# Building the second mixer's bias tables from GpSimd's queue in the second feed-forward block instead of from SyncE's in the first

## The chip, the cores and the metric

The kernel runs on one core of a Trainium2 chip. The metric is the device time of one execution in microseconds; before the change it is 2590.12 us, the median of three runs (2588.21 to 2591.35).

A core has five engines that run side by side, each taking its own instructions in a fixed order: TensorE (PE, with its weight loads as PEld), VectorE (DVE), ScalarE (ACT), GpSimd (POOL) and SyncE (SP), which here only starts transfers. Sixteen DMA engines move the data. A transfer is started by an instruction in the queue of SyncE, ScalarE or GpSimd, and an engine that comes to an instruction whose input has not arrived waits, with everything behind it.

## What is computed

A trunk of two layers over 768 tokens (512 of a prompt, 256 of a sample) of width 1024, all in float32:

```python
def swiglu(h, wg, wu, wd):
    return (jax.nn.silu(h @ wg) * (h @ wu)) @ wd

def even_layer(x, ...):
    x = x + 0.5 * swiglu(rmsnorm(x, f1_n), f1_g, f1_u, f1_d)
    x = x + mixer_ab(rmsnorm(x, mix_n), ...)     # gMLP gate and windowed attention
    return x + 0.5 * swiglu(rmsnorm(x, f2_n), f2_g, f2_u, f2_d)

def odd_layer(x, ...):                           # the same two feed-forward blocks
    ...
    x = x + mixer_c(rmsnorm(x, mix_n), w_qkv, rpb, w_out)
    ...

def neighbourhood_attn(q, k, v, rpb):
    ...
    dr = rs + jnp.arange(kh) - r + (NA_KH - 1)
    bias = rpb[:, dr][:, :, dc]
    s = jnp.einsum('bchd,bacjhd->bhcaj', q_row, k_win) * (HEAD_DIM ** -0.5)
    s = s + jnp.transpose(bias, (0, 2, 1, 3))[None]
    ...
```

The hidden width of the feed-forward blocks is 2816. The second mixer attends to a neighbourhood in a grid of 64 columns and adds a relative position bias `rpb` (16 heads, 15 x 31 values). The bias depends only on an input of the program, not on anything computed.

## The kernel before

**Stages.** `build` runs six phases one after the other: the feed-forward blocks l0f1, l0f2, l1f1 and l1f2, and between them the first mixer (after l0f1) and the second (after l1f1). In the profiled execution l0f1 runs until about 520 us, the first mixer to about 805, l0f2 to about 1260, l1f1 to about 1740 and the second mixer to about 2130.

**A feed-forward block** (`ffn`) takes the hidden width in 11 pairs of 256 columns (numbered 0 to 10). Each product of two matrices is made as seven products of half-size blocks, of sums and differences of the blocks, in place of eight. The sums of weight blocks are made on VectorE (`sums`, line 739, tile `s`). Every weight block then becomes a rounded part `whi` and a remainder `wlo` (`wsplit`, lines 122 and 123, on ScalarE and VectorE), and three matrix products (line 152) take the place of one in full precision. The order of a block is: the first two products of pairs 0 to 3, then the rest of pair 0, 1, 2 and so on. After pair 2 comes `down` for pairs 0 and 1, the product with the down weights, whose results are accumulated into `x` by VectorE (line 795); then pairs 3 and 4, `down` for 2 and 3, and so on.

**Weights** are loaded by `raw` (line 107) in tiles of 512 KB, from SyncE's queue, into four buffers. A load can start once an earlier tile in the same buffer has been read for the last time. For pairs 0 to 3 of each block, one of the weight sums is built by the transfers themselves: `added` starts two loads into the same tile `s` on GpSimd's queue, the second of which adds to what the first has written (`accum_op`). There are 16 such loads in each block, 8 plain and 8 accumulating.

**The bias tables.** The second mixer wants the bias laid out by query position. `bias_tables` (line 1621) builds that with transfers from DRAM to DRAM, in two steps for the prompt and two for the sample: 16 shifted copies of `rpb` into `skew`, 8 strided copies from `skew` into `tab`, then 32 and 4 of the same for the sample, 60 in all. A copy into `skew` moves 16 x 15 pieces of 32 or 48 numbers (30 or 45 KB); a copy into `tab` moves 16 x 16 pieces of 1 KB or 16 x 32 pieces of 768 bytes. `bias_tables` does not start them; it puts them on a list, `spare`, when `build` comes to the first phase. `raw` starts one of them, on SyncE's queue, behind each weight load from the twentieth on (lines 108 and 109), so all of them stand among the loads of l0f1. What were left of the list would be started ahead of the second mixer (lines 1710 and 1711). `mixer1` reads the tables head by head (line 1423).

**What sets the order.** TensorE's instructions are in the order of the program, written out by hand. Those of the other engines are ordered by Tile's planner when the kernel is built, from priorities and from when it expects their operands to be there. `issue_after(ins)` puts what is traced within it behind `ins` on that engine's queue. `mixed` is true in the feed-forward blocks that follow a mixer, l0f2 and l1f2.

Of the kernel before, what the change touches and what calls it, by code (L numbers as in the profile page):

```python
# [55 lines left out]
class Trunk:  # L56
# [42 lines left out]
    def raw(self, name, k0, nk, c0, n, raw=None, eng=None, **kw):  # L99
        i = len(self.units)  # L100
        self.units.append((name, k0, nk, c0, n))
        size = P * nk * n
        src = self.aps["w"][self.woff : self.woff + size].rearrange("(p f) -> p f", p=P)
        self.woff += size
        if raw is None:
            raw = self.rawp.tile([P, nk * n], F32, tag="raw", name=f"raw{i}")
        (eng or self.nc.sync).dma_start(raw, src, **kw)  # L107
        if self.spare and i >= 20:
            self.spare.pop(0)()
        return raw.rearrange("p (k n) -> p k n", k=nk)  # L110

    def wsplit(self, src, eng=None, keep=False):
# [365 lines left out]
    def ffn(self, pre):  # L478
# [4 lines left out]
        mixed = bool(self.unfed)  # L483
# [229 lines left out]
        for p in range(NPAIR):  # L713
            for _ in stages[p]:
                pass
            if p == 2:
                acc += [self.fw.tile([P, H], F32, tag=f"p1{j}", name=f"p1{j}") for j in range(4)]
            if p and p % 2 == 0 and p < NPAIR - 1:
                self.down(pre, range(p - 2, p), d, acc, addeds.get(p + 1))
            if p == NPAIR - 2:  # L720
                self.down(pre, range(p - 1, p), d, acc)
        kind = self.following[0]
# [898 lines left out]
    def bias_tables(self):  # L1621

        dma = self.nc.sync.dma_start
        rpb = self.aps["rpb"]
        self.tabs = []
        for nc_, nr, ns in ((16, 8, 32), (32, 4, 48)):
            skew = self.dram.tile([nc_, 16, 15, ns], F32, tag=f"skew{ns}", name=f"skew{ns}")
            tab = self.dram.tile([16, P, nr * ns], F32, tag=f"tab{ns}", name=f"tab{ns}")  # L1630
            self.tabs.append(tab)
            for c in range(nc_):
                self.spare.append(
                    lambda skew=skew, c=c, ns=ns: dma(skew[c], rpb[:, :, RPB_PAD + 7 - c : RPB_PAD + 7 - c + ns])
                )
            for r in range(nr):
                src = skew.rearrange("c h d s -> h c (d s)")[:, :, (7 - r) * ns : (7 - r + nr) * ns]
                dst = tab.rearrange("h (c r) f -> h r c f", r=nr)[:, r]
                self.spare.append(lambda dst=dst, src=src: dma(dst, src))

    def build(self):
        nc = self.nc
        space = self.cp.tile([P, 96], F32, tag="space", name="space")
        todo = [KIND[p] for p in self.phases] + [("last", 6)]
        kind = todo[0][0]
        self.ident = self.cp.tile([P, P], F32, tag="ident", name="ident")
        self.ones = self.cp.tile([P, P], F32, tag="ones", name="ones")
        self.onesr = self.cp.tile([P, P], F32R, tag="onesr", name="onesr")
        if kind == "f":
            pre = f"{self.phases[0][:2]}_ffn{self.phases[0][3]}_w_"  # L1650
            raws = [self.rawp.tile([P, KD * P], F32, tag="raw", name=f"first{i}") for i in range(4)]
            self.first += [t.rearrange("p (k n) -> p k n", k=KD) for t in raws]

            def first(i, k, eng=None):
                name = pre + ("gate", "up")[i % 2]
                self.raw(name, 4 * k, 4, i // 2 * 2 * P, P, raws[i][:, k * 512 : k * 512 + 512], eng)

            first(0, 0, nc.scalar)
        nc.gpsimd.memset(self.ones, 1.0)
        nc.vector.tensor_copy(self.onesr, self.ones)  # L1660
        self.space = space
        self.silu()
        make_identity(nc, self.ident)
        self.gains = self.cp.tile([P, 64], F32, tag="gains", name="gains")[:, : KD * len(NORMS)]
        nc.scalar.dma_start(self.gains, self.aps["gains"])
        self.ngains = self.cp.tile([P, 64], F32, tag="ngains", name="ngains")[:, : KD * len(NORMS)]
        nc.gpsimd.tensor_scalar(out=self.ngains, in0=self.gains, scalar1=-1.0, scalar2=None, op0=ALU.mult)
        self.x = [self.xp.tile([P, T], F32, tag=f"x{m}", name=f"x{m}") for m in range(KD)]
        if kind == "f":
            self.ffn_open("right")  # L1670
            self.ffn_tiles()
            self.fw = self.open("work", "left")
            self.early = {}
            for h in (0, 1):
                self.spawn(self.tok_norm(h))
        elif kind != "last":
            self.mixer_tiles("right")
        self.norm_begin(todo[0])
        self.mixed = False
        if kind == "f":  # L1680
            ps = self.psum(self.aux, "aux")
            for _ in range(WARM):
                nc.tensor.matmul(ps[:, :P], lhsT=self.onesr, rhs=self.onesr, start=True, stop=True)
        for h, (c0, c1) in enumerate(HALVES):
            for m in range(KD):
                nc.sync.dma_start(self.x[m][:, c0:c1], self.aps["x"][m, :, c0:c1])
                if kind == "f":
                    if h == 0:
                        self.feed(m, 0)
                else:  # L1690
                    self.final(m, c0, c1)
                if h == 0 and m % 4 == 3 and kind == "f":
                    for i in range(4):
                        if m > 4 or i:
                            first(i, m // 4)
            if kind == "f":
                for _ in range(TOKQ[h]):
                    self.tok_load()
                if h:
                    self.spawn(self.second())  # L1700
            elif kind == "last":
                self.half_done(h)
            if kind == "last":
                self.drain()
        for i, ph in enumerate(self.phases):
            self.following = todo[i + 1]
            if i == 0 and "l1m" in self.phases:
                self.bias_tables()
            if ph == "l1m":
                while self.spare:  # L1710
                    self.spare.pop(0)()
            if ph == "l0m":
                self.mixer0()
            elif ph == "l1m":
                self.mixer1()
            else:
                self.ffn(f"{ph[:2]}_ffn{ph[3]}")
        self.drain()
        for n in list(self.guards)[::-1]:
            self.close(n)  # L1720
# [105 lines left out]
```

## Time and profile before

| | us |
|---|---|
| median of three runs | 2590.12 |
| lowest and highest | 2588.21, 2591.35 |
| the profiled execution, its time | 2590.38 |
| the profiled execution, its span (first to last instruction) | 2588.6 |

The mean granted TensorE clock of the profiled execution is 0.996 of full speed. Its page gives the busy time of each engine over the whole span, and the mean hides what single stages do: the first block, which holds the transfers in question, has to be read by itself, in a table of windows, in the chain of work that ended last, and in the timelines of single engines. In a timeline row stand the start, the length, the engine, the line, the operation, what it writes and reads, and in brackets the idle time ahead of it with the work that ended it.

### The profile page before, as it was taken

How to read it: one execution, taken by the hardware profiler on the slowest of the kernel's cores; microseconds unless marked ns; L12 is line 12 of the kernel's file. 1: busy time of each engine (PE TensorE's matmuls, PEld its weight loads, DVE VectorE, ACT ScalarE, POOL GpSimd, SP SyncE). 2: the span in 40 equal slices, each digit the busy share in tenths (PEclk: the TensorE clock that was granted, in tenths of full speed). 3: DMA queues.
4: the chain of work that ended last, by engine and by line, in shares of the span. 5: the costliest groups of instructions: out<-in, count | busy, mean ns of one | idle time of the engine just before them, and what ended most of it. 6: DMA issues, size and time to landing. Idle time of an engine off the chain costs nothing.

```text
span 2588.6 us, 41317 instructions
## 1 busy us (share of the span) xinstructions
PE 2552.2 (99%) x15114; PEld 2487.2 (96%) x15114; DVE 2232.6 (86%) x4662; ACT 1366.6 (53%) x2869; POOL 155.5 (6%) x252
## 2 busy tenths in 40 slices
PE   8999999999999999999999999999999999999998
PEld 8999999988899999999999999998998999999997
DVE  7988898978879989889998889886776699888897
ACT  7544454646656545445654445454455575444543
POOL 1000000000021000000100000001222220000000
PEclk9999999999999999999999999999999999999999
DMA  7523222331144322222542222242221343222222
GB/s 246 170 81 106 72 74 74 124 100 46 58 125 132 114 66 74 74 66 98 136 109 82 66 77 71 66 145 64 64 64 41 106 134 119 82 74 74 71 66 76
DMA packets 93372, 238.68 MB, mean 92 GB/s; under 512 B 21488, under 2 KB 34288, under 8 KB 93168
## 3 DMA queue, kind: packets, MB, share of 16 engines
q1 hardware_dynamic: 85712, 218.96, 26.3%
q0 software_dynamic: 7168, 16.78, 3.1%
q8 instruction: 119, 1.95, 0.3%
q14 instruction: 85, 0.70, 0.1%
q10 hardware_dynamic: 288, 0.29, 0.0%
HBM read 226.56 MB, written 15.07 MB: 93 GB/s over the span
## 4 chain that ended last, share of the span: by engine, by line
PE 89%; DVE 6%; ACT 2%; DMA 1%; issue 1%; SPq 0%; DVEq 0%; ACTq 0%
PE ps_mm L152 54%; PE ps_aux L152 34%; PE ps_aux L156 1%; DVE wlo L123 1%; ACT p L1109 1%; DVE p L1103 1%; DMA raw<-in_w 1%; DVE tl L209 0%; DMA x<-in_x 0%; DVE tmp L415 0%; DVE p L1119 0%; ACT whi L122 0%; DVE s L739 0%; DMA first<-in_w 0%; DVE o L1254 0%
## 5 line engine op out<-in xcount | busy, mean ns | idle before, releaser
L122 ACT CAST whi<-s 128x512 fp32r<-128x512 f32 x496 | 304.6, 620 | 407.3 <-DVE s L739 177.6
L122 ACT CAST whi<-raw 128x512 fp32r<-128x512 f32 x504 | 306.1, 619 | 222.9 <-PE ps_mm L152 91.3
L123 DVE TENSOR_TENSOR wlo<-s,whi 128x512 fp32r<-128x512 f32 x496 | 336.8, 684 | 61.0 <-ACT whi L122 53.4
L123 DVE TENSOR_TENSOR wlo<-raw,whi 128x512 fp32r<-128x512 f32 x471 | 321.7, 691 | 18.2 <-ACT whi L122 14.5
L152 PE MATMUL ps_mm<-db,whi 128*128 128x384 f32 x864 | 219.2, 334 | 0.0
L152 PE MATMUL ps_aux<-dt,whi 128*128 128x384 f32 x864 | 219.2, 334 | 0.0
L152 PEld LDWEIGHTS ps_aux<-dt,whi 128*128 128x128 f32 x864 | 156.0, 188 | 0.0
L152 PEld LDWEIGHTS ps_mm<-db,whi 128*128 128x128 f32 x864 | 156.0, 188 | 0.0
L152 PE MATMUL ps_mm<-xh,whi 128*128 128x512 f32 (+1 forms) x416 | 146.2, 352 | 0.0
L152 PE MATMUL ps_aux<-dt,wlo 128*128 128x384 f32 x432 | 144.4, 334 | 1.4 <-DVE wlo L123 1.4
L152 PE MATMUL ps_mm<-db,wlo 128*128 128x384 f32 x432 | 144.3, 334 | 0.0
L152 PE MATMUL ps_mm<-xh,wlo 128*128 128x512 f32 (+1 forms) x416 | 141.3, 340 | 0.0
L152 PE MATMUL ps_mm<-xl,whi 128*128 128x512 f32 (+1 forms) x416 | 141.2, 339 | 0.0
L739 DVE TENSOR_TENSOR s<-raw,raw 128x512 f32<-128x512 f32 x124 | 84.0, 685 | 25.7 <-DMA raw<-in_w 25.5
L578 DVE TENSOR_TENSOR u<-ps_aux,u 128x384 f32<-128x384 f32 x176 | 96.9, 550 | 4.9 <-PE ps_aux L152 4.8
L152 PE MATMUL ps_aux<-dh,whi 128*128 128x384 f32 x384 | 97.5, 334 | 0.0
L795 DVE TENSOR_TENSOR x<-ps_aux,x 128x384 f32<-128x384 f32 x160 | 85.3, 551 | 14.1 <-PE ps_aux L152 13.8
L1109 ACT ACTIVATE p<-p,st 128x256 f32<-128x256 f32 (+3 forms) x144 | 68.9, 480 | 49.3 <-DVE st L1107 49.2
L573 ACT COPY u<-ps_mm 128x384 f32<-128x384 f32 x176 | 83.5, 475 | 16.5 <-PE ps_mm L152 15.9
L795 DVE TENSOR_TENSOR x<-ps_mm,x 128x384 f32<-128x384 f32 x160 | 86.1, 550 | 7.1 <-PE ps_mm L152 6.8
L107 POOL DMA_DIRECT2D s<-in_w x64 | 47.1, 781 | 702.2 <-PE ps_aux L152 387.6
L152 PEld LDWEIGHTS ps_mm<-xh,whi 128*128 128x128 f32 x416 | 79.8, 192 | 9.3 <-issue 0.9
(516 smaller groups left out, 8134.1 us busy)
## 6 DMA issues: line engine op xcount, KB each, us to landing
raw<-in_w SPq DMA_DIRECT2D x346, 512.0 KB, 3.7
s<-in_w POOLq DMA_DIRECT2D x64, 256.0 KB, 5.0
xdm<-x SPq DMA_DIRECT2D x16, 384.0 KB, 2.4
x<-in_x SPq DMA_DIRECT2D x16, 192.0 KB, 6.3
tok<-in_xt SPq DMA_DIRECT2D x12, 256.0 KB, 6.5
xold<-xdm SPq DMA_DIRECT2D x8, 384.0 KB, 3.1
x<-xdm SPq DMA_DIRECT2D x8, 384.0 KB, 4.7
out_y<-y SPq DMA_DIRECT2D x8, 384.0 KB, 2.4
```

Source lines behind the costliest of these rows:

```text
L107: (eng or self.nc.sync).dma_start(raw, src, **kw)
L122: nc.scalar.copy(hi, src)
L123: (eng or nc.gpsimd).tensor_tensor(out=lo, in0=src, in1=hi.bitcast(F32), op=ALU.subtract)
L152: self.nc.tensor.matmul(out, lhsT=lhsT, rhs=rhs, start=start, stop=stop, **kw)
L156: self.nc.tensor.transpose(out, src, self.ident)
L573: nc.scalar.copy(e[n, out], bank[key, n])
L578: nc.vector.tensor_tensor(out=t, in0=bank[key, n], in1=t, op=ALU.add)
L739: f = lambda o, x, y, op: self.nc.vector.tensor_tensor(out=o, in0=x, in1=y, op=op)
L795: nc.vector.tensor_tensor(out=o, in0=ps, in1=o, op=ALU.add)
L1103: nc.vector.tensor_tensor_reduce(out=outs[i], in0=ps_list[i], in1=adds[i], scale=1.0, scalar=init[i], op0=ALU.add, op1=ALU.max, accum_out= ...
L1109: ins = nc.scalar.activation(outs[i], outs[i], AF.Exp, bias=nm[:, i : i + 1], accum_out=sm[:, i : i + 1])
```

## The change

```diff
@@ raw
-        (eng or self.nc.sync).dma_start(raw, src, **kw)
-        if self.spare and i >= 20:
-            self.spare.pop(0)()
+        ins = (eng or self.nc.sync).dma_start(raw, src, **kw).ins
+        if kw:
+            self.added = ins
         return raw.rearrange("p (k n) -> p k n", k=nk)
@@ ffn, in the loop over the pairs
             if p and p % 2 == 0 and p < NPAIR - 1:
                 self.down(pre, range(p - 2, p), d, acc, addeds.get(p + 1))
+                if mixed and p == 2 and self.spare:
+                    with self.tc.issue_after(self.added):
+                        while self.spare:
+                            self.spare.pop(0)()
@@ bias_tables
-        dma = self.nc.sync.dma_start
+        dma = self.nc.gpsimd.dma_start
@@ build
-            if ph == "l1m":
-                while self.spare:
-                    self.spare.pop(0)()
```

`raw` no longer starts transfers of the list; it keeps the last accumulating load in `self.added` (only such a load has a `kw`). In the first block with `mixed` true, which is l0f2, the whole list is started in one go behind the `down` of pairs 0 and 1, on GpSimd's queue and there behind the last accumulating load of pair 3, the last that the block has. The loop ahead of the second mixer goes. The 60 transfers themselves, what they read and write and their order among each other stay as they are; a copy into `tab` still waits for the copies into `skew` that it reads.

## The prediction

> **What bounds the kernel now.** I read the first part of the page, then the groups, for the engines and the price of a transfer on GpSimd's queue.
>
> ```profile
> span 2588.6 us, 41317 instructions
> PE 2552.2 (99%) x15114; PEld 2487.2 (96%) x15114; DVE 2232.6 (86%) x4662; ACT 1366.6 (53%) x2869; POOL 155.5 (6%) x252
> ...
> L107 POOL DMA_DIRECT2D s<-in_w x64 | 47.1, 781 | 702.2 <-PE ps_aux L152 387.6
> ```
>
> TensorE is busy for 2552.2 of 2588.6 us, so a change without TensorE work can only gain where TensorE stands still or runs slowly. The next view, of the two tiles `skew` and `tab`, says where the moved transfers are now and when their product is first read.
>
> ```profile
> L1634 SPq DMA_DIRECT2D skew<-in_rpb x48: 490/604/782, 42.7 to 227.3; - x48
> L1639 SPq DMA_DIRECT2D tab<-skew x12: 531/562/751, 76.5 to 272.9; - x12
> ...
> L1423 SPq DMA_DIRECT2D ba<-tab x16: 320/326/468, 1739.5 to 1961.6; - x16
> ```
>
> There are 60 transfers, issued between 42.7 and 272.9 us, all inside the first feed-forward block (l0f1), and the tables are first read at 1739.5. So I looked for lost TensorE time between 40 and 300, in the table of windows (window; length; busy us and count of PE, PEld, DVE, ACT, POOL; granted clock; DMA share; GB/s):
>
> ```profile
> 40.00:60.00 20.00, 18.69 (x104) 17.54 (x102) 19.75 (x51) 18.40 (x45) 2.91 (x4) 1.00 0.52 122
> 60.00:80.00 20.00, 19.40 (x111) 19.08 (x111) 19.73 (x41) 10.06 (x22) 2.95 (x4) 1.00 0.70 182
> ...
> 140.00:160.00 20.00, 16.10 (x81) 14.89 (x80) 13.37 (x24) 7.11 (x14) 0.00 (x0) 0.91 0.31 88
> ...
> 280.00:300.00 20.00, 18.55 (x108) 18.23 (x107) 18.02 (x35) 8.90 (x19) 0.00 (x0) 1.00 0.18 53
> ```
>
> Four windows lose something. Idle time alone misses part of it: at 140 to 160 the granted clock is 0.91 as well. A better measure is a twin. The three feed-forward blocks l0f1, l0f2 and l1f1 send the same products in the same order from their first `down` on, and l0f2 and l1f1 have none of the 60 transfers. From the chain of work that ended last (start, length, what), the same places in l0f1, then l0f2, then l1f1:
>
> ```profile
> 121.72 8.32 PE ps_mm L152 x48
> ...
> 173.76 16.64 PE ps_mm L152 x96
> ...
> 277.76 8.32 PE ps_aux L152 x48
> ...
> 296.13 8.32 PE ps_mm L152 x48
> ...
> 866.80 8.32 PE ps_mm L152 x48
> ...
> 912.56 16.71 PE ps_mm L152 x96
> ...
> 1353.88 8.32 PE ps_mm L152 x48
> ...
> 1399.64 16.64 PE ps_mm L152 x96
> ...
> 1503.64 8.32 PE ps_aux L152 x48
> ...
> 1520.28 8.32 PE ps_mm L152 x48
> ```
>
> From the first mark to the second, l0f1 takes 173.76 - 121.72 = 52.04 us, l0f2 912.56 - 866.80 = 45.76 and l1f1 1399.64 - 1353.88 = 45.76: l0f1 loses **6.28 us**. From the third to the fourth it takes 18.37, l1f1 16.64: it loses **1.73 us**. Together 8.01.
>
> Why are they lost? First suspicion: the weight loads come late because SyncE is busy with the small transfers. SyncE's timeline at the first loss, in l0f1 and, 1232.16 us later, in l1f1:
>
> ```profile
> 135.55 0.33 SPq L107 DMA_DIRECT2D raw<-in_w  x1
> 135.93 0.52 SPq L1634 DMA_DIRECT2D skew<-in_rpb  x1
> 139.14 0.33 SPq L107 DMA_DIRECT2D raw<-in_w  x1
> ...
> 1367.71 0.33 SPq L107 DMA_DIRECT2D raw<-in_w  x1
> ...
> 1371.29 0.33 SPq L107 DMA_DIRECT2D raw<-in_w  x1
> ```
>
> That suspicion falls. 1367.71 - 1232.16 = 135.55 and 1371.29 - 1232.16 = 139.13: both loads leave at the same relative time. VectorE's timeline shows what does differ:
>
> ```profile
> 144.64 0.56 DVE L795 TENSOR_TENSOR x<-ps_aux,x 128x384 f32<-128x384 f32 x1 [0.48 <-PE ps_aux L152]
> 145.12 0.68 DVE L739 TENSOR_TENSOR s<-s,raw 128x512 f32<-128x512 f32 x1
> ...
> 290.76 0.68 DVE L739 TENSOR_TENSOR s<-s,raw 128x512 f32<-128x512 f32 x1
> ...
> 1371.32 0.69 DVE L739 TENSOR_TENSOR s<-s,raw 128x512 f32<-128x512 f32 x1
> ...
> 1512.82 0.68 DVE L739 TENSOR_TENSOR s<-s,raw 128x512 f32<-128x512 f32 x1
> ```
>
> In l1f1 the weight sum runs at 1371.32, which is 3.61 us after its load was issued. In l0f1 it runs at 145.12, 9.57 us after the load, and the last thing ahead of it is an accumulation that itself waited 0.48 us for TensorE. VectorE takes its instructions in a fixed order, and here that order has the sum behind products that TensorE had yet to finish: 145.12 - (1371.32 - 1232.16) = 5.96 us late. The second loss has the same form: 290.76 in l0f1 is 13.00 us after its mark, 1512.82 in l1f1 is 9.18 after. So the loss is **order**, not a missing load. VectorE's order comes from Tile's planner, which places an instruction when it expects the operands. My reading is that it expected the loads of this stretch later because 60 transfers stood in their queue.
>
> **The change part by part.** *Taken from SyncE:* 60 issues, between 42.7 and 272.9. Their issue time (about 0.6 us each, 36 us in all) is worth nothing by itself, since the loads next to them leave when their buffer comes free, as in the twin. What goes is the reason for the late order. I value that at the twin's distance, 6.28 + 1.73 = 8.01 us. Bounds: nothing if the order stays, and beyond 8.01 the windows 40:60 and 60:80. At the twin's rate (16.64 us for 96 matmuls, 0.1733 each) 20 us hold 115.4; they hold 104 and 111, which is 15.8 too few, 2.7 us. VectorE is busy 19.75 and 19.73 of 20 there, so the start is limited by its work and I take 0 for it; a new order can give or cost up to those 2.7.
>
> *Put on GpSimd:* the same 60 issues behind the last accumulating load of l0f2. GpSimd's timeline shows that load and what follows it:
>
> ```profile
> 853.49 1.82 POOL L107 DMA_DIRECT2D s<-in_w  x2 [3.27 <-DMA s<-in_w]
> 1239.90 1.12 POOL L107 DMA_DIRECT2D s<-in_w  x2 [384.59 <-PE ps_aux L152]
> ```
>
> The burst can start at 855.3, and the next instruction behind it comes at 1239.90, after 384.59 idle us. No row shows such a transfer on this queue. The nearest is the load of 128 pieces at 0.781 us. At that price 60 take 47 us. If the price goes by pieces, a `skew` transfer has 16 x 15 = 240 of them, a `tab` transfer 256 (eight) or 512 (four): 48 x 1.46 + 8 x 1.56 + 4 x 3.12 = 95 us. I take the middle, some 70 us; the burst ends between 902 and 951, waits for landings added. A `tab` transfer waits for its `skew` transfers, and behind the waiting one stand only others of the 60. Cost 0, hidden by the 384.59 us; without that cover the loads of 1239.90 would be late by what sticks out. Table readers have until 1739.5.
>
> *In the queues past which it moves:* the burst meets l0f2's weight loads. What do the transfers take of the DMA engines? The DMA view of 160 to 280 (l0f1), then of 902 to 1022 (l0f2), both with 16 weight loads:
>
> ```profile
> q1 hardware_dynamic: 11064, 11.13, 32.0%
> ...
> raw<-in_w SPq DMA_DIRECT2D x16, 512.0 KB, 3.6
> tab<-skew SPq DMA_DIRECT2D x4, 384.0 KB, 4.6
> skew<-in_rpb SPq DMA_DIRECT2D x25, 45.0 KB, 3.6
> ...
> q1 hardware_dynamic: 2175, 7.93, 21.4%
> ...
> raw<-in_w SPq DMA_DIRECT2D x16, 512.0 KB, 3.6
> ```
>
> (32.0 - 21.4)% of 120 us is 12.7 us for 29 transfers, 0.44 each, so some 26 us for 60. In a burst of 47 to 95 us that is a share of 0.28 to 0.56 on top of 0.21. The loads' median landing was 3.6 us with and without the 29 between them, so the nearest row says that contention costs nothing; the burst is 2.6 to 5.3 times as dense. How little room there is, the waits of VectorE and the sum of its windows over 855 to 975 say:
>
> ```profile
> DVE s L739 <- DMA raw<-in_w: 5.9, 6, 2.9
> ...
> sum 120.00, PE 120.00 PEld 119.59 DVE 106.97 ACT 59.18 POOL 0.31; mean PE 20.00 PEld 19.93 DVE 17.83 ACT 9.86 POOL 0.05
> ```
>
> Six sums already wait for a load (5.9 us), and VectorE idles 120 - 106.97 = 13.03 us in all, so 7.1 us can absorb later loads. I take 0 between a gain of 0 and the 14.5 us worked out below.
>
> The sum: 2590.4 us (the profiled execution: the span of 2588.6 and 1.8 around it) - 8.0 - 0 - 0 = 2582.4. The median of the runs shown, 2590.12, lies 0.3 lower, so I say **2582.1 us**.
>
> **The rivals.** *The late order moves with the transfers.* If the planner lets transfers of any queue delay the loads that it expects, the sums of l0f2 that meet the burst come late in VectorE's order instead. Pair 3's sum (the one that l0f1 has at 145.12) falls at 1371.32 - (1353.88 - 866.80) = 884.24, in the burst. For it: the same code. Against it: a transfer on another queue stands ahead of no weight load. Price: the same 8.0, net 0, 2590; denser by 60 to 29, it could be worse.
>
> *The order has another cause.* l0f1 also starts from loads of its own, with other due times, and VectorE is full until 100 us. Then nothing comes back: 2590. Against it: the second loss is at 290, long after the start, and just behind the last `tab` transfer at 272.9. It is also the form in which the change does as it says and that doesn't matter.
>
> *Slower: the two queues share the DMA engines and the weight loads of l0f2 land late.* Until now the small transfers stood in the loads' own queue, one or a few behind a load; in the burst they come from a second queue at any time. If a load then lands twice as late (3.6 us more) at each of the six sums that already wait, 21.6 us less the 7.1 of cover make 14.5, and with the gain of 8.0 the kernel takes 6.5 longer: 2597. It decides from (8.0 + 5.2 + 7.1) / 6 = 3.4 us a load. Against it are the equal 3.6 us above; for it only the burst's density. [...]
>
> **How the numbers follow.** This kernel's measurement tells about 0.2%, 5.2 us, from no change. Forecast 0.58, order moves 0.17, other cause 0.13, shared engines 0.12. The forecast's own range is 2579.5 (with the start's 2.7) to 2585.5 (only the 6.28, less a little contention); 0.05 of it falls within 0.2%, so faster has 0.53. Same: 0.05, the other cause's 0.13 and 0.12 of the moved order, 0.30. Slower: the shared engines' 0.12 and 0.05 of a moved order in a denser burst, 0.17. The range runs from 2578.5 to 2593: it takes in the cases with no net change and leaves out most of the slower rival.
>
> **What would show it.** Right: pair 3's sum in l0f1 runs about 3.6 us after its load, the first two marks are 45.8 us apart and the next two 16.6; 60 transfers on GpSimd's queue from 855 less the gain, done before 960; l0f2's marks still 45.8 apart. Wrong: marks in l0f1 unchanged (another cause); VectorE's sum behind accumulations in l0f2 (the order moved); more than 5.9 us of waits for loads and landings well over 3.6 us there (shared engines). A change of order in the mixers, or in the first 100 us, by more than 2.7 us, would make the sum wrong in a way none of the cases prices.

## The result, and the profile after

| | before | after |
|---|---|---|
| median, us (19 runs each) | 2591.06 | 2585.46 |
| lowest and highest, us | 2588.21, 2594.55 | 2582.47, 2590.84 |
| profiled execution, time, us | 2590.38 | 2586.14 |
| profiled execution, span, us | 2588.6 | 2584.4 |

The ratio after / before is 0.9978, interval 0.9972 to 0.9985: the change saves 5.6 us, 0.22%. The prediction was 2582.1 within 2578.5 to 2593.0.

The first part of the page of after: TensorE's busy time is within 1 us of what it was. GpSimd has 60 more instructions.

```profile
span 2584.4 us, 41339 instructions
PE 2553.1 (99%) x15114; PEld 2487.8 (96%) x15114; DVE 2229.9 (86%) x4662; ACT 1365.8 (53%) x2869; POOL 189.0 (7%) x312
```

The chain that ended last in after has the same marks in l0f1 as the prediction read (start, length, what), then the long product near the end of l0f1's `down` (x240), then the first two marks of l0f2:

```profile
119.64 8.32 PE ps_mm L152 x48
...
165.40 16.64 PE ps_mm L152 x96
...
269.40 8.32 PE ps_aux L152 x48
...
286.04 8.32 PE ps_mm L152 x48
...
462.84 41.60 PE ps_aux L152 x240
...
860.95 8.32 PE ps_mm L152 x48
...
906.71 16.64 PE ps_mm L152 x96
```

The first stretch now takes 165.40 - 119.64 = 45.76 us and the second 286.04 - 269.40 = 16.64, exactly the twins' figures, and l0f2's own first stretch stays at 906.71 - 860.95 = 45.76. In before the long product stands here:

```profile
472.93 41.60 PE ps_aux L152 x240
```

So the profiled execution of after is 472.93 - 462.84 = 10.1 us ahead at that mark (2.1 of it already at the first mark), but only 866.80 - 860.95 = 5.9 at l0f2's first mark. Between the two lies the first mixer: 393.87 us in before, 398.11 in after. What was won in the block was partly lost again in a stage that the change does not touch. The window that showed the loss before, 140 to 160, and one of l0f2 with the burst in it (columns as in the prediction) are full in after:

```profile
140.00:160.00 20.00, 20.00 (x117) 20.00 (x116) 19.14 (x37) 12.24 (x25) 0.00 (x0) 1.00 0.30 106
865.00:885.00 20.00, 20.00 (x117) 20.00 (x116) 16.98 (x33) 9.39 (x19) 16.70 (x31) 1.00 0.80 205
```

The moved transfers, from the views of the tiles `skew` and `tab` in after (duration of one issue in ns, lowest/median/highest, then first and last start), and GpSimd's timeline at the end of the burst:

```profile
L1638 POOL DMA_DIRECT2D skew<-in_rpb x48: 562/562/984, 849.4 to 889.3; - x48
L1643 POOL DMA_DIRECT2D tab<-skew x12: 567/612/661, 864.8 to 898.8; - x12
```

```profile
898.79 0.63 POOL L1643 DMA_DIRECT2D tab<-skew  x1 [2.03 <-issue]
1233.70 1.12 POOL L107 DMA_DIRECT2D s<-in_w  x2 [334.27 <-PE ps_aux L152]
```

The burst runs from 849.4 to 899.4 and 334 idle us are left behind it. It does load the DMA engines. Their view of 845 to 905 in after, then VectorE's waits over 845 to 965, then the landings of the tile `raw` in 845 to 905 and, at the same place of before, in 851 to 911:

```profile
q0 software_dynamic: 3072, 6.69, 45.3%
q1 hardware_dynamic: 1511, 5.47, 27.2%
```

```profile
DVE s L743 <- DMA raw<-in_w: 5.7, 7, 1.6
```

```profile
DMA to landing us min/median/max: 3.7/4.2/6.4
...
DMA to landing us min/median/max: 3.5/4.1/6.7
```

GpSimd's queue (q0) takes 45.3% of the DMA engines' time over these 60 us and the weight loads' (q1) 27.2%. The nine weight loads issued there land in 4.2 us at the median, against 4.1 for the nine at the same place before. VectorE waits 5.7 us for loads, where it waited 5.9 in the same place before.

### The profile page after: what moved, and what is told of

It is laid out like the page before. It is cut to its first block, busy times and chain, and to the rows that moved or that the text cites. A ratio compares the mean times of both kernels' runs of the same rounds, so it can differ in the third digit from the quotient of the medians.

```text
span 2584.4 us, 41339 instructions
## 1 busy us (share of the span) xinstructions
PE 2553.1 (99%) x15114; PEld 2487.8 (96%) x15114; DVE 2229.9 (86%) x4662; ACT 1365.8 (53%) x2869; POOL 189.0 (7%) x312
## 4 chain that ended last, share of the span: by engine, by line
PE 83%; DVE 11%; DMA 2%; ACT 2%; issue 1%; SPq 0%; DVEq 0%; ACTq 0%
PE ps_mm L152 50%; PE ps_aux L152 32%; DVE wlo L123 2%; DMA raw<-in_w 1%; DVE s L743 1%; PE ps_aux L156 1%; ACT p L1113 1%; DVE p L1107 1%; DVE tmp L415 1%; DVE tl L209 0%; DMA first<-in_w 0%; DVE p L1123 0%; DVE u L578 0%; DVE o L1258 0%; DMA x<-in_x 0%
## 5 line engine op out<-in xcount | busy, mean ns | idle before, releaser
L123 POOL TENSOR_TENSOR wlo<-raw,whi 128x512 fp32r<-128x512 f32 x33 | 43.9, 1337 | 715.9 <-DVE p L1123 583.8
L573 ACT COPY u<-ps_mm 128x384 f32<-128x384 f32 x176 | 83.4, 474 | 10.3 <-PE ps_mm L152 10.1
```

The costliest lines, as they stand in the source:

```text
L123: (eng or nc.gpsimd).tensor_tensor(out=lo, in0=src, in1=hi.bitcast(F32), op=ALU.subtract)
L573: nc.scalar.copy(e[n, out], bank[key, n])
```

## The experiments

Two theories stood after the first reading. **Order**: transfers in the loads' own queue made the planner place VectorE's weight sums too late in l0f1. **Load**: the transfers themselves, beside the weight loads of the first block, cost the time. For the first, the prediction had one instruction, the sum at 145.12.

**The gate sum held back.** On the kernel after, no transfer moved: the first weight sum of pair 3 (of the gate weights) is put behind the accumulation that stood ahead of it in before.

```diff
 def entry():
     load((0, 1))
-    return parts("gate", "t2")
+    with self.tc.issue_after(self.sums_of[1]) if p == EARLY - 1 and len(self.sums_of) == 4 else nullcontext():
+        return parts("gate", "t2")
...
```

The part left out records the accumulations of the `down` products in `sums_of`.

> The changed kernel with one more ordering edge: in the first block, pair 3's first weight sum stands on VectorE's queue behind the second accumulation of the last product of the first down, where the kernel before had it. No transfer is moved. Stretch A is the time between the first two marks of the prediction (52.04 us before, 45.76 in the changed kernel), stretch B between the other two (18.37 before, 16.64 changed). Theory (order alone costs the time): A is 51 to 52.5, B stays 16.64, the median about 6 us above the changed kernel's, near 2591. Rival (the transfers beside the weight loads cost it): A stays 45.8 and the time that of the changed kernel, 2585.5.

Measured: 2585.19 us, ratio to before 0.9976 (0.9967 to 0.9985), the same as after. VectorE's timeline and the chain:

```profile
143.42 1.28 DVE L745 TENSOR_TENSOR s<-s,raw 128x512 f32<-128x512 f32 x2
```

```profile
120.03 8.32 PE ps_mm L153 x48
...
166.55 16.64 PE ps_mm L153 x96
```

The gate sum is as late as in before (143.42 - 120.03 = 23.39 us after the mark; before 145.12 - 121.72 = 23.40), and the stretch takes 46.52, only 0.76 more than in after. The prediction had picked the wrong instruction. Two sums of pair 3 have the form `s<-s,raw`, one for the gate weights and one for the up weights. Both are in VectorE's timeline of before in l0f1, and in after and in l1f1 of before; the buffer numbers in the program tell which is which:

```profile
145.12 0.68 DVE L739 TENSOR_TENSOR s<-s,raw 128x512 f32<-128x512 f32 x1
...
151.36 0.68 DVE L739 TENSOR_TENSOR s<-s,raw 128x512 f32<-128x512 f32 x1
...
1351.12 0.69 DVE L739 TENSOR_TENSOR s<-s,raw 128x512 f32<-128x512 f32 x1 [0.21 <-DMA raw<-in_w]
...
1371.32 0.69 DVE L739 TENSOR_TENSOR s<-s,raw 128x512 f32<-128x512 f32 x1
```

```profile
118.75 0.69 DVE L743 TENSOR_TENSOR s<-s,raw 128x512 f32<-128x512 f32 x1
...
137.54 0.69 DVE L743 TENSOR_TENSOR s<-s,raw 128x512 f32<-128x512 f32 x1 [0.52 <-DMA raw<-in_w]
```

In l0f1 of before 145.12 is the gate sum and 151.36 the up sum; in l1f1 they are 1351.12 and 1371.32, and the trace has 1371.32 released by the load of 1367.71, the twin of 135.55. The load of 135.55 feeds the *up* sum, so the sum ran 151.36 - 135.55 = 15.8 us after its load's issue, 12.2 us later than in l1f1, not the 5.96 of the prediction, which had set the gate sum of one block against the up sum of the other. In after the order is that of the twin.

The row of this run is marked x2: the up sum stands right behind the gate sum, at 144.02, which is 23.99 us after the mark. So the run delays the up sum too, by 6.1 us against after (137.54 - 119.64 = 17.90), and even both sums behind the accumulations cost no more than 0.76. In before the up sum stands 29.64 us after the mark and behind one thing more. VectorE's and TensorE's timelines of before there:

```profile
150.29 0.56 DVE L209 TENSOR_TENSOR db<-sg,db 128x384 fp32r<-128x384 f32 x1 [1.97 <-ACT db L208]
...
152.81 0.45 PE L152 MATMUL ps_mm<-t20h,whi 128*128 128x384 f32 x1 [3.47 <-ACT whi L122]
```

VectorE idles 1.97 us for the split at 150.29, whose input comes from ScalarE and, one step before, from the products that TensorE has just made. Only then comes the up sum, at 151.36, and TensorE stands still for 3.47 us until the first rounded part made from that sum is there.

**Transfers on GpSimd's queue, but still in the first block.** On the kernel before, one word changed. This parts the queue from the place.

```diff
-        dma = self.nc.sync.dma_start
+        dma = self.nc.gpsimd.dma_start
```

> The kernel before with one word changed: the 60 transfers are still started behind the first block's weight loads in the program, but on GpSimd's queue. They move beside the same loads, and the order on VectorE differs from the changed kernel's only in some rows of the first 120 us. Theory (the planner delays a sum only for transfers in the loads' own queue): A 45.8 and B 16.6, the time within 3 us of the changed kernel's, so the place in the second block is not needed. Rival (transfers beside the loads cost the time, whatever their queue): A 50 or more, the time that of the kernel before, 2591.

Measured: 2586.45 us, ratio 0.9981 (0.9972 to 0.9990). The tile views, then the chain:

```profile
L1634 POOL DMA_DIRECT2D skew<-in_rpb x48: 560/567/1190, 1.3 to 126.1; - x48
L1639 POOL DMA_DIRECT2D tab<-skew x12: 569/754/957, 41.8 to 133.0; - x12
```

```profile
120.55 8.32 PE ps_mm L152 x48
...
166.31 16.64 PE ps_mm L152 x96
...
270.31 8.32 PE ps_aux L152 x48
...
286.95 8.32 PE ps_mm L152 x48
```

All 60 transfers run beside the first block's loads, and the stretches are 45.76 and 16.64. The queue alone brings the gain, and moving to the second block adds nothing measurable to it. The theory **load** is weakened, but not settled by this run: on GpSimd's queue the transfers are over at 133 us, and the time lost in before lies between 140 and 160 and behind 277. The last experiment settles the first of the two places.

**Transfers on SyncE's queue, but in the second block.** On the kernel after, the transfers go back to SyncE, behind the last weight load that SyncE has issued by then.

```diff
-        if kw:
+        if eng is None:
             self.added = ins
...
-        dma = self.nc.gpsimd.dma_start
+        dma = self.nc.sync.dma_start
```

> The changed kernel with the burst on SyncE's queue, in the second block, behind the last weight load ahead of it. Theory (own queue): A 45.8 and B 16.6 in the first block as in the changed kernel, and the late order turns up in the second block, where the stretch that is A's twin (45.76 in both kernels) becomes 50 or longer, since the burst of 60 is denser and also holds up real loads behind it; time 2591 to 2600. Rival (the place in the program matters, not the queue): the twin stays 45.8 and the time is that of the changed kernel.

Measured: 2599.84 us, ratio 1.0034 (1.0022 to 1.0046): 8.8 us slower than before and 14.4 slower than after. l0f1 is good (45.76 and 16.64). l0f2 is not: by TensorE's timeline its first stretch takes 63.5 us. SyncE's timeline, VectorE's, and the windows of this kernel:

```profile
843.86 13.03 SPq L1638 DMA_DIRECT2D skew<-in_rpb  x17
858.12 5.13 SPq L1643 DMA_DIRECT2D tab<-skew  x8
863.29 22.33 SPq L1638 DMA_DIRECT2D skew<-in_rpb  x31
885.71 1.02 SPq L107 DMA_DIRECT2D raw<-in_w  x2
```

```profile
883.71 0.56 DVE L799 TENSOR_TENSOR x<-ps_aux,x 128x384 f32<-128x384 f32 x1 [0.49 <-PE ps_aux L152]
890.66 0.69 DVE L743 TENSOR_TENSOR s<-s,raw 128x512 f32<-128x512 f32 x1 [6.40 <-DMA raw<-in_w]
```

```profile
870.00:890.00 20.00, 13.67 (x79) 13.35 (x78) 8.41 (x15) 3.51 (x7) 0.00 (x0) 0.90 0.50 100
890.00:910.00 20.00, 13.80 (x51) 12.92 (x52) 12.48 (x21) 7.24 (x14) 0.00 (x0) 0.68 0.71 246
```

Here the loss is not order alone. The late order has come along with the transfers: the sum stands behind the last accumulation, at 883.71. But the loads are late as well: from 843.86 to 885.71 SyncE issues 56 transfers in one go and no weight load, and the sum that the loads feed waits 6.40 us for them. Read this as the first suspicion of the prediction: late loads, false in l0f1, where one transfer stood behind each load, and true for a burst in the same queue. The run does not part the two.

**No transfers.** The 60 transfers are left out of the kernel after, and the second mixer loads parts of its mask, of the same size, where it would load the tables.

```diff
-                self.bias_tables()
+                pass
...
-            for t, tab in zip((ba, bb), self.tabs):
-                nc.sync.dma_start(t.rearrange("p a c -> p (a c)"), tab[h])
+            for t, n in zip((ba, bb), (256, 192)):
+                nc.sync.dma_start(t.rearrange("p a c -> p (a c)"), self.aps["nmask"][:, :n])
```

> The changed kernel without the 60 transfers; the second mixer loads parts of its mask as stand-ins for the tables, so its output is not the reference's. Theory (the burst in the second block costs nothing): A, B and A's twin as in the changed kernel, the time within 2 us of it. Rival (the burst costs what is missing between the 10 us won in the first block and the 5.6 us of the medians): faster than the changed kernel by 3 to 5 us, near 2581. For all four runs: from the start of the first block's last long product (240 matmuls) to the second block's first mark took 393.87 us in the profile before and 398.11 in the one after. If the clock that falls at different moments of the first mixer makes this difference, it varies by some us from run to run with no tie to the edit; if the change makes it, it is near 398 wherever the first block is short and near 394 in e1.

Measured: 2584.54 us, ratio 0.9975 (0.9965 to 0.9985). That is 0.9 us below after, and the intervals of the two overlap almost wholly: no cost of the burst can be told from nothing, and l0f2's first stretch is 45.76 with it and without it.

**Both sums held back.** With the first experiment's edit, the up sum too is put where before had it, behind a split of VectorE that comes after the second product of the pair. Again no transfer moves.

```diff
+                    late = i == 0 and p == EARLY - 1 and len(self.sums_of) == 4
...
-                        st = parts(*todo[i + 1])
+                        if not late:
+                            st = parts(*todo[i + 1])
...
                         keep(b.replace("t", "u"), "Y", n)
+                        if late:
+                            with self.tc.issue_after(self.split_of):
+                                st = parts(*todo[i + 1])
```

> E1 put only the sum of pair 3's gate weights late and lost 0.8 us of the 6.3. This one puts the sum of its up weights late as well, behind the split that stands ahead of it in the kernel before; VectorE's rows there are then those of the kernel before, and no transfer is moved. Theory (order alone): stretch A 50 to 52.5, B 16.64, the median 4 to 6 us above the changed kernel's. Rival (the transfers beside the loads are needed too): A at most 48.

Measured: 2590.75 us, ratio 1.0003 (0.9993 to 1.0012). VectorE's timeline, the chain and the window:

```profile
143.11 0.68 DVE L750 TENSOR_TENSOR s<-s,raw 128x512 f32<-128x512 f32 x1
...
148.75 0.69 DVE L750 TENSOR_TENSOR s<-s,raw 128x512 f32<-128x512 f32 x1
```

```profile
119.72 8.32 PE ps_mm L153 x48
...
172.10 16.64 PE ps_mm L153 x96
```

```profile
140.00:160.00 20.00, 17.02 (x79) 15.69 (x79) 13.98 (x26) 7.32 (x14) 0.00 (x0) 0.83 0.31 106
```

The stretch takes 172.10 - 119.72 = 52.38, as in before, and the whole gain is gone with the transfers still on GpSimd's queue in l0f2. So no transfer has to stand beside the loads, and **load** falls for the first stretch. **Order** is shown there: with the up sum 29.0 us after the mark, behind the split, the loss is whole; with it 24.0 us after the mark, ahead of the split, it is 0.76. The up sum was not held back alone, and other instructions of VectorE move with it.

The second stretch keeps its 16.64 in this run, so its 1.7 us are not shown in the same way. They go in every kernel that has no transfers on SyncE's queue in l0f1. The trace of before fits order there too: the last load before the sum at 290.76 was issued at 281.44 and had landed at 285.84. But no run put that order back alone.

**Where the rest of the 8 us went.** The profiled execution of after is 4.2 us faster, not 8.0. More executions of both kernels were profiled, to tell what belongs to the kernel from what belongs to one execution. In the texts that follow, A and B are the first and the second stretch, and the offset is that of the clock's grid, explained below the table.

> The kernel before once more, for the parts of its time. Theory (clock): A is not 52.04 in every execution, since 1.6 us of its loss were matmuls at the lower clock after the idle time; without that A is near 50. The first mixer (from the start of the first block's last long product to the second block's first mark) took 393.87 in the first profile; theory: it varies by some us between executions, up to 398 here too. Rival (the change lengthens the mixer): within 1 us of 393.9 again.

> The changed kernel once more. A 45.76, B 16.64 and A's twin in the second block 45.76 again, since nothing idles there. The first mixer anywhere from 393 to 398 if the clock decides; within 1 us of 398.1 if the change does.

> As for the first look: A between 50 and 52, the first mixer anywhere from 393 to 398 if the clock decides, within 1 us of 393.9 if the change does.

> In the profiles so far every stretch at half clock lasts 3.4 us or a multiple, costs 1.7 us per 3.4, and starts on a grid of 3.413 us whose offset is constant within an execution: 3.1, 0.2, 2.9 and 2.6 in the executions with a long first block, 1.1, 0.6, 0.9, 1.5 and 1.7 in those with a short one. The first mixer had 1 or 2 such stretches in the former and 1 to 4 in the latter. Theory (the grid runs freely, the groups are chance): offsets of this and the next three looks fall anywhere, and the first mixer of the changed kernel has 1 or 2 low stretches where its offset is like those before. Rival (offset or number belongs to the kernel): offset 0.6 to 1.7 again and 2 to 4 stretches.

> Theory (free grid): an offset that may fall between 0.6 and 2.4, and then more than 2 low stretches in the first mixer are possible. Rival: an offset between 2.6 and 0.2 (through 3.4) again, and 1 or 2 stretches.

> As for the second look at the changed kernel: under the free grid any offset and a first mixer of 391 us plus 1.7 for each low stretch; under the rival an offset of 0.6 to 1.7 and 2 to 4 stretches.

> As for the third look at the kernel before: under the free grid any offset, and a first block whose loss changes with the number of low stretches in it; under the rival an offset between 2.6 and 0.2 and 1 or 2 stretches in the first mixer.

Their times were 2590.95, 2593.59, 2590.09 and 2589.74 us for before, and 2582.67, 2587.50 and 2586.98 for after. Marks from the chain of each (in the rows with a star the chain does not pass l0f2's first mark, and TensorE's timeline gives it); "mixer" is from the long product in l0f1 to l0f2's first mark, "low" the number of 3.4-us stretches at half clock in it, "rest" from that mark to the end of the span, "phase" the time from the last point of the clock's grid to the long product:

| | first mark | 1st stretch | 2nd | long product | phase | mixer | low | rest |
|---|---|---|---|---|---|---|---|---|
| before | 121.72 | 52.04 | 18.37 | 472.93 | 2.2 | 393.87 | 2 | 1721.8 |
| before, second | 121.25 | 52.26 | 18.38 | 472.69 | 1.5 | 392.73 | 1 | 1723.7 |
| before, third | 119.82 | 52.84 | 18.39 | 471.85 | 1.3 | 394.58 | 1 | 1725.4 |
| before, fourth | 119.01 | 52.24 | 18.36 | 470.41 | 1.8 | 394.60 | 2 | 1723.2 |
| before, fifth | 119.67 | 51.79 | 18.39 | 470.65 | 2.5 | 394.30 | 1 | 1723.0 |
| both sums late* | 119.72 | 52.38 | 16.64 | 469.54 | 2.8 | 393.51 | 1 | 1723.6 |
| after | 119.64 | 45.76 | 16.64 | 462.84 | 1.0 | 398.11 | 4 | 1723.4 |
| after, second | 120.10 | 45.76 | 16.64 | 463.30 | 1.9 | 394.81 | 2 | 1722.7 |
| after, third | 121.38 | 45.76 | 16.64 | 464.58 | 0.1 | 397.40 | 3 | 1723.6 |
| after, fourth | 120.83 | 45.76 | 16.64 | 464.03 | 0.7 | 396.72 | 4 | 1724.4 |
| gate sum late | 120.03 | 46.52 | 16.64 | 463.99 | 2.3 | 397.08 | 4 | 1724.2 |
| GpSimd, first block | 120.55 | 45.76 | 16.64 | 463.75 | 1.5 | 392.78 | 1 | 1722.8 |
| SyncE, second block* | 119.70 | 45.76 | 16.64 | 462.90 | 0.3 | 395.81 | 3 | 1739.4 |
| no transfers | 119.06 | 45.76 | 16.64 | 462.26 | 3.2 | 396.06 | 3 | 1723.1 |

From the five before to the four after the mean of the long product's start falls by 8.0 us (471.7 to 463.7), all of it from the two stretches (6.5 and 1.7): the first mark has not moved beyond its scatter. The mixer's mean grows by 2.7 (394.1 to 396.8), and the rest is the same (1723.4, 1723.5). 8.0 - 2.7 is 5.3, beside the medians' 5.6.

The first stretch has low clock in it as well. All five executions of before, and the one with both sums late, have one or two low stretches there, so a part of the 6.5 us (some 1.7 in four of the five) is lower clock that followed the idle time (in before a granted clock of 0.50 from 153.28 to 156.69, where the matmuls set in again behind the idle 3.47 us). An execution without one, in which the first stretch was expected near 50, was not seen.

What the mixer loses is clock. Windows of 2 us, first of before, then of after:

```profile
582.00:584.00 2.00, 1.76 (x11) 1.18 (x11) 1.66 (x6) 1.39 (x2) 0.00 (x0) 0.84 0.00 0
584.00:586.00 2.00, 2.00 (x11) 1.70 (x9) 1.79 (x6) 1.86 (x4) 0.00 (x0) 0.50 0.00 0
586.00:588.00 2.00, 2.00 (x16) 2.00 (x16) 1.73 (x7) 1.54 (x3) 0.00 (x0) 0.81 0.00 0
```

```profile
586.00:588.00 2.00, 0.78 (x5) 0.57 (x6) 1.93 (x8) 1.97 (x4) 0.00 (x0) 1.00 0.00 0
588.00:590.00 2.00, 2.00 (x11) 2.00 (x12) 2.00 (x4) 0.00 (x0) 0.00 (x0) 0.54 0.00 0
590.00:592.00 2.00, 2.00 (x12) 2.00 (x11) 2.00 (x7) 0.00 (x0) 0.00 (x0) 0.50 0.02 8
...
596.00:598.00 2.00, 2.00 (x5) 1.61 (x6) 1.71 (x8) 0.42 (x1) 0.00 (x0) 0.50 0.00 0
598.00:600.00 2.00, 2.00 (x9) 1.60 (x9) 0.93 (x3) 1.16 (x5) 0.00 (x0) 0.90 0.14 8
```

The granted clock falls to 0.50 for one stretch in before and for three in a row in after (588.1 to 598.4), each time behind a moment in which TensorE stood still for part of its time, here 0.78 busy of 2.00. In the 3.41 us just ahead of the first low stretch of a row in the mixer TensorE was busy for 2.32 and 1.97 us in before (stretches at 583.36 and 634.56) and 1.24 and 1.97 in after (588.14 and 629.10), and its longest pause there was 0.62 to 1.66 us. By windows of 2 us it was busy for 1.2 to 3.0 us at the same place in the other executions; for the one with the transfers on SyncE's queue in the second block there are only windows of 5 us, too wide to tell. The second and the third stretch of the row in after follow one in which TensorE was busy throughout (3.41 of 3.41). The order of instructions in the mixer is the same in both kernels, and before has such pauses too. Within an execution all low stretches begin on one grid with a period of 3.41 us (in after at 588.14 and 629.10, which is 12 periods later), and the grid's offset differs between executions. At a granted clock of 0.50 a low stretch costs by estimate up to half its length, 1.7 us (in before TensorE starts a matmul of 128x384 every 0.32 us between 154.26 and 156.18, every 0.18 between 156.94 and 157.83). Before has 1.4 of them on average and after 3.25, and 1.85 x 1.7 = 3.1 us, beside the 2.7 that the mixer grew. Their number does not say all: with one the mixer took 392.7 to 394.6 us.

Why after meets the grid less well is not fully settled. The grid's offset, counted from the start of the span, does not belong to the kernel: in the four executions of after it is 1.1, 0.6, 0.2 and 2.6, in the five of before 3.1, 0.2, 2.9, 1.0 and 0.5. But it was not as expected either: at offsets like those of before (0.2 and 2.6), for which 1 or 2 low stretches were expected, after had 3 and 4. A possible reason is that l0f1's loss itself contains a low stretch (the clock of 0.91 at 140 to 160; 0.50 from 153.28 to 156.69), which ends on a grid point, so that all that follows starts in step with the grid; without it the mixer starts anywhere. The column "phase" bears this out: the six executions with the long first stretch reach the long product 1.3 to 2.8 us behind a grid point, the eight without it anywhere. Nine executions lie between 1.3 and 2.8, and in eight of them the mixer takes 392.7 to 394.8 us, whichever kernel it is; in the five others it takes 395.8 to 398.1. The one exception is the run with the gate sum late (2.3, 397.08). So the reason is likely, but it was read from these executions afterwards; no run set the phase.

## Why the prediction was right, point by point

**The gain in l0f1: right in size, right in cause, wrong in its witness.** The twin's distance, 6.28 + 1.73 = 8.01 us, came out as 8.0. That the loss of the first stretch was VectorE's order and not late loads is shown by the run with both sums late. The step that compared 145.12 with 1371.32 set a gate sum against an up sum; the sum that matters stands at 151.36, and what it waits behind is the split at 150.29, not the accumulations. That the step's conclusion, order, held all the same is luck. It cost the forecast nothing because the value was taken from the marks, not from that difference. For the 1.73 of the second stretch the size is shown and the cause is argued. Why the planner orders VectorE so is a reading too: that the queue of the transfers decides it is shown by the kernel before with one word changed; that the planner expects the loads later is not shown.

**The start: 0, right.** The two us between the first marks of the first two profiles (121.72, 119.64) are scatter: before has 119.0 to 121.7 in its five, after 119.6 to 121.4 in its four.

**The burst on GpSimd: 0, right.** It took 50 us, near the lower of the two bounds (47 and 95), and not the middle, 70: 562 ns for an issue of 240 pieces, where a load of 128 pieces took 781 on average; 33.5 us for all (GpSimd's busy time, 189.0 against 155.5), and the rest waits. So a price by pieces does not hold here.

**The shared DMA engines: 0, right.** The median landing beside the burst, 4.2 us, is 0.1 us above that at the same place before, and the waits did not grow (5.7 us, before 5.9); the slower rival needed 3.4 us a load. Two more runs bear on it: the kernel without transfers (2584.54 us, beside 2585.46), and the one with all of them in the first block (2586.45 us). That a load lands twice as late beside transfers of a second queue, the 3.6 us of the rival's 14.5, is shown by no run: with 45.3% beside 27.2% of the engines' time the loads landed 0.1 us later.

**The two rivals without a gain: fallen.** On GpSimd's queue the order did not move with the transfers (l0f2's first stretch stays 45.76, in one execution 46.07, and with the transfers on that queue beside the first block's loads the gain is the same); on SyncE's queue it did. It had no other cause: one word, the queue, brings it back to the twin's.

**What was missing: 2.7 us.** The forecast was 3.4 us too low. Its sum has no term for the first mixer. It named a change of more than 2.7 us in the mixers as what no case prices, but thought of order; the order stayed and the granted clock changed (low stretches in the mixer, on average: 1.4 before, 3.25 after). 2582.1 + 2.7 and the 0.9 by which the median of all runs of before lies above the 2590.12 used make 2585.7, beside the 2585.46 measured. The range held it, the forecast's own range (2579.5 to 2585.5) just.

## What to carry to other kernels

A small transfer in the queue of the large loads cost time here without delaying a load (6.5 us on average in l0f1's first stretch): the planner that orders the other engines placed the readers of those loads late, presumably because it expected the loads later. Put it on a queue on which nothing near is waited for (GpSimd's had 334 idle us behind the burst); don't send many in one go on the loads' queue: 56 of them, from 843.86 to 885.71, delayed the loads in earnest here (a sum waited 6.40 us, and the kernel took 14.4 us longer than with the burst on GpSimd's queue). Value such a change by the same stretch in a twin stage, and check with the program's buffer names that two rows are the same instruction before subtracting them. Allow a few microseconds for stages that come after: here the next one lost clock (2.7 us on average), probably by starting at another moment.

## What the runs showed of the hardware that was not expected

- TensorE's granted clock fell to 0.50 in whole stretches of 3.41 us on a grid that was fixed within an execution (588.14 and 629.10 in after) and differed between executions (offsets of 0.2 to 3.1 us). In the first mixer alone 1 to 4 such stretches were seen in executions with the same order of instructions there, by estimate up to 1.7 us each, and its time went from 392.7 to 398.1 us. The pauses of TensorE ahead of the first of a row were short: 0.62 to 1.66 us in before and after, where TensorE was busy for 1.24 to 2.32 us of the 3.41 ahead.
- An issue on GpSimd's queue took 0.56 us for a transfer of 240 pieces and 0.61 at the median for the copies into `tab`, with more and larger pieces: nearly one price (0.57 and 0.75 in the run beside the first block's loads).
- Two queues that together held 72.5% of the DMA engines' time over 60 us (45.3% and 27.2%) left the median landing of a 512 KB load at 4.2 us, against 4.1 at the same place without the burst.
